# Walking the streamed operand of an MLP's matmuls in interleaved pieces

## Chip, cores and metric

The kernel runs on one core of a Trainium2 chip. The metric is the device time of one execution in microseconds. Two executions of the kernel before took 1046.23 and 1046.22 us, median 1046.22 us. Besides these there is one profiled execution, from which all rows come.

## What is computed

A trunk of two layers over 512 tokens with 1024 features, in float32. Layer 0 mixes by multi-head latent attention, layer 1 by gated linear attention; each mixer is followed by an MLP with a squared ReLU, and every part adds to the residual stream.

```
def sq_relu_mlp(xn, w_up, w_down):          # w_up 1024 x 4096, w_down 4096 x 1024
    hid = jnp.square(jax.nn.relu(xn @ w_up))
    return hid @ w_down

for i in range(2):
    x = x + mixer_i(rms_norm(x, norm_mix[i]))
    x = x + sq_relu_mlp(rms_norm(x, norm_mlp[i]), mlp_w_up[i], mlp_w_down[i])
return rms_norm(x, final_norm)
```

The change touches the MLP alone, in both layers.

## The kernel before

*Numbers in two parts.* Each float32 operand is split into a high part, which the matmul's input type holds, and a low part, the rest. A product is then three matmuls: high by high, high by low and low by high. ScalarE makes the high part (line 110), VectorE the low one (line 113); for weights both are called from `piece`, which writes them to the tiles `wh` and `wl`.

*Steps.* The 4096 hidden features of an MLP are taken in eight blocks of 512. The first block's hidden values are made by `up_first`. Then seven steps follow, b = 0 to 6: step b makes the hidden values of block b + 1 (the up products) and multiplies those of block b by their part of `w_down` (the down products). The last block's down product comes after the loop. Step 0 is `step`, which alternates up and down products; steps 1 to 6 are `step_in_halves`, which makes all up products first and then all down products.

*Seven products in place of eight.* Each block product of 2 by 2 quarters is made by seven quarter products of sums and differences of quarters, which VectorE, ScalarE and the accumulating DMAs form. So a step has seven calls of `up_product` and seven of `down_product`.

*`up_product`* (line 956 on) holds a quarter of `w_up` in the array, 128 columns at a time, and streams 256 tokens of the activations past it: two halves j, four k, three terms, 24 matmuls of 256 columns, all issued in line 962. The sums of half j lie in columns j x 256 and on of one bank of the sums' memory.

*`down_product`* (line 965 on) holds 128 tokens of the hidden values and streams 512 columns of `w_down`: two groups of tokens, two k, three terms, 12 matmuls of 512 columns, all issued in line 971. The sums fill one bank each.

In each matmul call the second argument is the operand that is held in the array (its load is a row of its own in the profile, PEld), and the third is the one that is streamed. The names after the arrow in a profile row have the streamed one first. Until now every streamed row and every row of sums was walked from its first column to its last.

*Order of the work.* TensorE runs its matmuls in the order of the program. The loads of `w_up` and `w_down` for the next step are issued by `fetch` on SyncE's queue, and for sums of two quarters on GpSimd's queue as well (lines 949 and 951), at places that `after` marks. Elsewhere in the program, the attention of layer 1 scales rows in place in groups of 1, 2, 4 and so on elements (line 1492, over the view `crossing` of line 1480) and copies such views (line 1541); these are among the rows that the prediction uses for comparison.

Of the kernel before, what the change touches and what calls it, by code (L numbers as in the profile page):

```python
# [50 lines left out]
def trunk_kernel(ctx: ExitStack, tc: tile.TileContext, t_in: dict, out: bass.AP):  # L51
    nc = tc.nc
    PE, ACT, DVE, POOL, SP = nc.tensor, nc.scalar, nc.vector, nc.gpsimd, nc.sync
# [22 lines left out]
    def bank(tag):  # L76
        return psum["pool"].tile([P, 512], F32, tag=f"ps_{tag}", bufs=psum["banks"][tag], name=uname("ps"))
# [72 lines left out]
    def piece(raw, a, n, order=lambda i: i, at=(W_AT, W_AT)):  # L150
        hi = room_for("wh", a, n, at[0])
        lo = room_for("wl", a, n, at[1])
        split(raw, hi, lo, order=order)
        return hi, lo

    def cut(pair, *idx):
        return tuple(t[idx] for t in pair)
# [657 lines left out]
    def mlp(layer, nrm, nxt=None):  # L815
# [3 lines left out]
        KH = ND // 2  # L819
# [112 lines left out]
        def fetch(b, name):  # L932
            if name in ("A1", "A2"):
                c = int(name[1]) - 1
                if c == 0:
                    W[name] = col_chunk(w_up, (b + 1) * FB, 256)
                    return None
                W[name] = t = sb.tile([P, ND, 256], F32, tag="wraw", bufs=2, name=uname("wraw"))
                SP.dma_start(t[:, :KH], up_quadrant(b, 1, 0))
                POOL.dma_start(t[:, :KH], up_quadrant(b, 0, 0), accum_op=ALU.add)  # L940
                SP.dma_start(t[:, KH:], up_quadrant(b, 1, 1))
                return None
            q = up_quadrant if name == "S1" else down_quadrant
            W[name] = t = by_k(comb(home[name]), KH if name == "S1" else 2)
            plain, more = {
                "d11": ((0, 0), None), "d12": ((0, 1), None), "d22": ((1, 1), None),
                "S1": ((1, 1), (1, 0)), "dS1": ((1, 1), (1, 0)), "dS3": ((1, 0), (0, 0)),
            }[name]
            first_part = SP.dma_start(t, q(b, *plain))
            if more:  # L950
                POOL.dma_start(t, q(b, *more), accum_op=ALU.add)
            return first_part

        def up_product(t, a, q, start):
            w = piece(a, KH, 256, at=AT_UP)
            for j in range(2):
                o = t[:, j * TH : (j + 1) * TH]
                for k in range(KH):
                    wh, wl = cut(w, slice(None), k, slice(j * P, (j + 1) * P))
                    xh, xl = quad[q][k][:, 0], quad[q][k][:, 1]  # L960
                    for n, (a_, x_) in enumerate(((wh, xh), (wh, xl), (wl, xh))):
                        PE.matmul(o, a_, x_, start=start and j == 0 and k == 0 and n == 0, stop=k == KH - 1 and n == 2, skip_group_check=True)  # L962

        def down_product(t, a, parts, start):
            wh, wl = piece(a, 2, 512)
            for tt in range(2):
                o = t[tt] if isinstance(t, list) else t[:, tt * 512 : (tt + 1) * 512]
                for k in range(2):
                    xh, xl = cut(parts, slice(None), slice(k * TH + tt * P, k * TH + (tt + 1) * P))
                    for n, (x_, w_) in enumerate(((xh, wh[:, k]), (xh, wl[:, k]), (xl, wh[:, k]))):  # L970
                        PE.matmul(o, x_, w_, start=start and k == 0 and n == 0, stop=k == 1 and n == 2, skip_group_check=True)  # L971


        def step(b, q, r, after):
# [14 lines left out]
            def onto(tag, total, a, parts, fresh=False):  # L989
                t = two_banks(tag)  # L990
                if not fresh:
                    ACT.activation(t, total, AF.Copy)
                down_product(t, a, parts, fresh)
                ACT.activation(total, t, AF.Copy)
# [4 lines left out]

            z = bank("u")  # L1000
            up_product(z, a11, "11", True)
            y = bank("u")
            ACT.activation(y, z, AF.Copy)

            d = two_banks("d")
            down_product(d, d11, parts_of_quad(q11), True)
            if opening:
                ACT.activation(S11, d, AF.Copy)
            e = two_banks("e") if opening else begun(d)

            up_product(y, a12, "21", False)
            finish(y, 0, 0, r)
            DVE.tensor_tensor(a11, s1, a11, ALU.add)

            down_product(e, d12, parts_of_quad(q21), opening)
            DVE.tensor_tensor(S11, e, S11, ALU.add)
            DVE.tensor_tensor(d11, ds1, d11, ALU.add)
# [11 lines left out]
            def up_t2():  # L1029
                up_product(z, a11, "T2", False)  # L1030
                u = part["u"] = tmp()
                ACT.activation(u, z, AF.Copy)
                DVE.tensor_tensor(a12, a11, a12, ALU.add)
# [147 lines left out]
        def before_next(name):  # L1181
            if name in ("d11", "S1", "d12", "dS3"):
                t = by_k(comb(home[name]), 2)
                SP.dma_start(t, x_kept[:, 2 * len(kept) : 2 * len(kept) + 2])
                kept.append(t)
            if name in ("A1", "A2"):
                last_raw.append(load(down_cols(len(last_raw)), 4, 512))
            if name == "dS1":
                DVE.tensor_tensor(S12, S12, S5, ALU.add)

        def at_the_end(name):
            if name in ("d11", "S1", "d12", "dS3"):
                i = len(last_raw)
                t = by_k(comb(home[name]), 2)
                k0 = (NB - 1) * FB + i % 2 * 256
                SP.dma_start(t, w_dn[k0 : k0 + 256, i // 2 * 512 : (i // 2 + 1) * 512].rearrange("(k p) n -> p k n", p=P))
                last_raw.append(t)
            if name == "dS1":
                DVE.tensor_tensor(S12, S12, S5, ALU.add)
                t = comb(home[name])  # L1200
                SP.dma_start(t, t_in["fin_row"].to_broadcast([P, D]))
                gain.append(t)
                rounded(0)

        for b in range(NB - 1):
            final = b == NB - 2

            def after(name, b=b, final=final):
                if final:
                    return before_next(name) if nxt else at_the_end(name)  # L1210
                fetch(b + 1, name)

            (step_in_halves if b else step)(b, Q[b % 2], Q[(b + 1) % 2], after)

        q = Q[(NB - 1) % 2]
        if nxt:
# [6 lines left out]
            for c in range(2):  # L1223
# [5 lines left out]
                for j, p in enumerate(ps_):  # L1229
                    for t in range(NT):  # L1230
                        o = t % 2 * 512 + j * P
# [26 lines left out]
        for c in range(2):  # L1258
            for th in (1, 0):
                total = (S11, S12, S21, SU)[2 * c + th]  # L1260
                if c == 0:
# [3 lines left out]
                    o = loaded[th]  # L1265
                for i in range(2):
                    cs = slice(i * 512, (i + 1) * 512)
                    if c:
                        o = bank("u")
# [529 lines left out]
    n_mix1 = Norm(ND, inv_dr, "mix", ND)  # L1799
    psum_layout("quad")  # L1800
    mlp(0, n_mlp0, n_mix1)
    psum_layout(False)
    Y, begun = gla(0, n_mix1, "B", "B")
# [3 lines left out]

    psum_layout("quad")
    mlp(1, n_mlp1)


# [46 lines left out]
```

## Time and profile before

| | |
|---|---|
| median of the runs | 1046.22 us |
| profiled execution, span from first to last instruction | 1044.9 us |
| middle steps of layer 0 (steps 1 to 6) | 245.9 to 474.8 us of the span |
| middle steps of layer 1 (steps 1 to 6) | 785.9 to 1015.0 us of the span |
| one middle step | 38.16 us, twelve of them |

The page gives busy time by engine; PE is TensorE's matmuls, PEld its loads of the held operand, DVE VectorE, ACT ScalarE, POOL GpSimd, and a q behind an engine's name its queue. The slices cut the span in 40 equal parts with the busy share in tenths. The chain is the work that ended last, followed back from the end. Matmuls overlap in the array, so the duration of a single row (390 ns for 512 columns, 275 ns for 256) is longer than the distance from one matmul to the next; the distance is read from the starts, or from how long a run of many takes.

### The profile page before, as it was taken

The page shows a single profiled execution, that of the slowest core. Times are in us where ns is not written, and L with a number is a line of the kernel's source. Part 1 is how long each engine was busy: PE and PEld are TensorE (multiplying, and loading weights), DVE is VectorE, ACT ScalarE, POOL GpSimd, SP SyncE. Part 2 cuts the span into 40 slices and gives each one's busy share as a digit, 9 for nine tenths or more (in the row PEclk, how much of TensorE's full clock was granted, in tenths as well). Part 3 has the DMA queues.
Part 4 walks back from the last instruction along what each step waited for, and adds up shares of the span by engine and source line. Part 5 has one row for each costly group of instructions (what it writes and reads, how often), then busy time and mean ns, then how long its engine had stood idle before and what let it go on. Part 6 is the DMA issues. An engine that isn't in the chain of part 4 may idle for free.

```text
span 1044.9 us, 15747 instructions
## 1 busy us (share of the span) xinstructions
PE 1035.0 (99%) x5966; PEld 903.9 (87%) x5966; DVE 876.9 (84%) x1340; ACT 696.8 (67%) x1122; POOL 114.3 (11%) x128
## 2 busy tenths in 40 slices
PE   9999999999999999999999999999999999999997
PEld 8788888899899899898888888888889989989986
DVE  7889977988989989989687399469798999898993
ACT  8667754577776776785445566555677677677784
POOL 8400010301101101000000000000011111110000
PEclk9999999999999999999999999999999999999999
DMA  7401235769878778644212222165488778778422
GB/s 232 122 21 41 81 95 147 224 166 215 216 191 202 178 203 202 161 136 126 77 55 82 87 74 75 48 162 147 95 241 201 185 202 198 194 191 191 111 81 81
DMA packets 120717, 149.98 MB, mean 144 GB/s; under 512 B 9568, under 2 KB 86368, under 8 KB 120512
## 3 DMA queue, kind: packets, MB, share of 16 engines
q1 hardware_dynamic: 96144, 117.76, 35.4%
q0 software_dynamic: 22400, 29.36, 18.0%
q10 hardware_dynamic: 2096, 1.84, 0.6%
q8 instruction: 47, 0.77, 0.3%
q14 instruction: 30, 0.25, 0.1%
HBM read 144.49 MB, written 4.19 MB: 142 GB/s over the span
## 4 chain that ended last, share of the span: by engine, by line
PE 94%; DVE 3%; ACT 2%; issue 0%; DMA 0%; ACTq 0%; SPq 0%; DVEq 0%
PE ps L971 25%; PE ps L962 25%; PE ps L118 10%; PE ps L120 10%; PE ps L119 10%; PE ps L1279 2%; PE ps L1240 2%; PE ps L1499 1%; PE ps L135 1%; PE ps L421 1%; PE ps L1626 1%; DVE wl L113 1%; PE ps L1766 0%; PE ps L1549 0%; PE ps L684 0%
## 5 line engine op out<-in xcount | busy, mean ns | idle before, releaser
L971 PE MATMUL ps<-wh,set 128*128 128x512 f32 x784 | 245.7, 390 | 0.3 <-ACT set L110 0.3
L110 ACT ACTIVATE wh<-wraw 128x1024 fp32r<-128x1024 f32 x139 | 146.4, 1056 | 110.2 <-PE ps L119 42.6
L113 DVE TENSOR_TENSOR wl<-wraw,wh 128x1024 fp32r<-128x1024 f32 x139 | 169.7, 1222 | 39.0 <-ACT wh L110 38.7
L971 PEld LDWEIGHTS ps<-wh,set 128*128 128x128 f32 x784 | 147.0, 188 | 30.7 <-ACT set L110 0.7
L962 PE MATMUL ps<-T,wh 128*128 128x256 f32 x896 | 154.9, 275 | 0.0
L971 PE MATMUL ps<-wl,set 128*128 128x512 f32 x392 | 152.6, 389 | 0.0
L113 DVE TENSOR_TENSOR wl<-comb,wh 128x1024 fp32r<-128x1024 f32 x112 | 136.8, 1221 | 18.5 <-ACT wh L110 18.3
L110 ACT ACTIVATE wh<-comb 128x1024 fp32r<-128x1024 f32 x112 | 118.3, 1057 | 47.6 <-issue 28.7
L962 PEld LDWEIGHTS ps<-T,wh 128*128 128x128 f32 x896 | 135.4, 188 | 0.4
L962 PE MATMUL ps<-T,wl 128*128 128x256 f32 x448 | 123.4, 275 | 0.0
L962 PE MATMUL ps<-set,wh 128*128 128x256 f32 x672 | 117.1, 276 | 0.0
L118 PE MATMUL ps<-set,wh 128*128 128x512 f32 x280 | 109.7, 392 | 0.0
L119 PE MATMUL ps<-set,wh 128*128 128x512 f32 x280 | 109.6, 392 | 0.0
L120 PE MATMUL ps<-set,wl 128*128 128x512 f32 x280 | 109.3, 391 | 0.0
L962 PEld LDWEIGHTS ps<-set,wh 128*128 128x128 f32 x672 | 102.6, 188 | 1.3
L962 PE MATMUL ps<-set,wl 128*128 128x256 f32 x336 | 92.7, 276 | 0.0
L971 PEld LDWEIGHTS ps<-wl,set 128*128 128x128 f32 x392 | 73.6, 188 | 14.7
L962 PEld LDWEIGHTS ps<-T,wl 128*128 128x128 f32 x448 | 84.1, 188 | 0.1
L962 PEld LDWEIGHTS ps<-set,wl 128*128 128x128 f32 x336 | 63.1, 188 | 0.0
L120 PEld LDWEIGHTS ps<-set,wl 128*128 128x128 f32 x280 | 52.6, 188 | 11.1
L119 PEld LDWEIGHTS ps<-set,wh 128*128 128x128 f32 x280 | 52.6, 188 | 11.1 <-DVE set L750 0.2
L118 PEld LDWEIGHTS ps<-set,wh 128*128 128x128 f32 x280 | 52.6, 188 | 10.7
(415 smaller groups left out, 2015.4 us busy)
## 6 DMA issues: line engine op xcount, KB each, us to landing
comb<-in_mlp_w_down_dram SPq DMA_DIRECT2D x74, 512.0 KB, 4.1
wraw<-in_mlp_w_up_dram SPq DMA_DIRECT2D x18, 1024.0 KB, 5.6
comb<-in_mlp_w_down_dram POOLq DMA_DIRECT2D x28, 512.0 KB, 6.5
wraw<-in_mlp_w_up_dram SPq DMA_DIRECT2D x28, 512.0 KB, 5.6
wraw<-in_gla_w_in_dram SPq DMA_DIRECT2D x12, 1024.0 KB, 5.2
comb<-in_mlp_w_up_dram SPq DMA_DIRECT2D x14, 512.0 KB, 4.4
comb<-in_mlp_w_up_dram POOLq DMA_DIRECT2D x14, 512.0 KB, 6.4
wraw<-in_mlp_w_up_dram POOLq DMA_DIRECT2D x14, 512.0 KB, 7.6
```

The lines of the kernel that those rows point to most:

```text
L110: order(ACT.activation(hi, src, AF.Copy))
L113: lo_eng.tensor_tensor(lo, src, f(hi), ALU.subtract)
L118: PE.matmul(psum, wh, xh, start=start, stop=False)
L119: PE.matmul(psum, wh, xl, start=False, stop=False)
L120: PE.matmul(psum, wl, xh, start=False, stop=stop)
L135: PE.transpose(psum, src, ident[: src.shape[0], : src.shape[0]])
L421: PE.matmul(p, w[:, i, j * P : (j + 1) * P], x, start=start, stop=stop)
L962: PE.matmul(o, a_, x_, start=start and j == 0 and k == 0 and n == 0, stop=k == KH - 1 and n == 2, skip_group_check=True)
L971: PE.matmul(o, x_, w_, start=start and k == 0 and n == 0, stop=k == 1 and n == 2, skip_group_check=True)
L1240: PE.matmul(p, a, x, start=False, stop=k == 3 and n == 2, skip_group_check=True)
L1279: PE.matmul(o, a, b_, start=False, stop=k == 3 and n == 2, skip_group_check=True)
L1499: PE.matmul(p[:, t - t0], k[:, t * P : (t + 1) * P], moving[:, t], start=True, stop=True)
```

## The change

A view `streamed` is put around the streamed operand and around the sums of both lines. With a pair (h, c) it cuts the row of N columns into h equal stretches and each stretch into N / (h c) pieces of c columns; the walk goes over the pieces in the outer loop, over the h stretches inside that, and over the c columns innermost. With the empty pair it leaves the row as it is. Each step sets its pair before it starts: step 0 has the empty one, steps 1 to 6 of layer 0 have (2, 16), (2, 32), (2, 8), (2, 4), (4, 16), (2, 64), and steps 1 to 6 of layer 1 have (4, 8), (8, 4), (8, 8), (8, 32), (2, 128), (16, 8).

```
+        ORDERS = (((), (2, 16), (2, 32), (2, 8), (2, 4), (4, 16), (2, 64)), ((), (4, 8), (8, 4), (8, 8), (8, 32), (2, 128), (16, 8)))[layer]
+        order = [()]
+
+        def streamed(ap):
+            if not order[0]:
+                return ap
+            h, c = order[0]
+            return ap.rearrange("p (h i c) -> p i h c", h=h, c=c)
+
         def up_product(t, a, q, start):
...
-                        PE.matmul(o, a_, x_, start=start and j == 0 and k == 0 and n == 0, stop=k == KH - 1 and n == 2, skip_group_check=True)
+                        PE.matmul(streamed(o), a_, streamed(x_), start=start and j == 0 and k == 0 and n == 0, stop=k == KH - 1 and n == 2, skip_group_check=True)
 
         def down_product(t, a, parts, start):
...
-                        PE.matmul(o, x_, w_, start=start and k == 0 and n == 0, stop=k == 1 and n == 2, skip_group_check=True)
+                        PE.matmul(streamed(o), x_, streamed(w_), start=start and k == 0 and n == 0, stop=k == 1 and n == 2, skip_group_check=True)
...
+            order[0] = ORDERS[b % len(ORDERS)]
             (step_in_halves if b else step)(b, Q[b % 2], Q[(b + 1) % 2], after)
```

The held operand of both lines, and every instruction outside them, is as before. The sums of each matmul land in the same places as before, since both views are walked alike.

## The prediction

> **What bounds the kernel now.** I read the page from the top: busy time by engine, the granted clock, then the chain that ended last.
>
> ```profile
> span 1044.9 us, 15747 instructions
> PE 1035.0 (99%) x5966; PEld 903.9 (87%) x5966; DVE 876.9 (84%) x1340; ACT 696.8 (67%) x1122; POOL 114.3 (11%) x128
> PEclk9999999999999999999999999999999999999999
> PE 94%; DVE 3%; ACT 2%; issue 0%; DMA 0%; ACTq 0%; SPq 0%; DVEq 0%
> PE ps L971 25%; PE ps L962 25%; PE ps L118 10%; PE ps L120 10%; PE ps L119 10%; PE ps L1279 2%; PE ps L1240 2%; PE ps L1499 1%; PE ps L135 1%; PE ps L421 1%; PE ps L1626 1%; DVE wl L113 1%; PE ps L1766 0%; PE ps L1549 0%; PE ps L684 0%
> ```
>
> TensorE is never without work, its clock is granted in full, and half of the chain runs through exactly two lines, L962 (the up products) and L971 (the down products). These are the two lines that the change edits. Whatever the new walk does to one of their matmuls goes into the end time without a cover.
>
> Next I asked for the chain of waits over the middle steps of the first layer, steps 1 to 6.
>
> ```profile
> by line: PE ps L971 50.1%; PE ps L962 50.0%
> 245.86 19.09 PE ps L962 x168
> 264.95 19.07 PE ps L971 x84
> 284.02 19.09 PE ps L962 x168
> 303.11 19.07 PE ps L971 x84
> 322.18 19.09 PE ps L962 x168
> ```
>
> A step is one unbroken run of 168 matmuls of 256 columns and then 84 of 512 columns; the next starts 38.16 us later (284.02 to 322.18). No other engine appears in this stretch. So the price of a column is the whole question. From these rows: 19.09 us / 168 = 113.6 ns for 256 columns and 19.07 us / 84 = 227.0 ns for 512, which is 0.443 ns for a column in both.
>
> The windows, one step each, say how near the others are (columns: stretch, sum, then busy time of PE, PEld, DVE, ACT, POOL, clock, DMA share, GB/s).
>
> ```profile
> core 0: us, PE busy (x) PEld busy (x) DVE busy (x) ACT busy (x) POOL busy (x), PEclk, DMA share, GB/s
> 283.85:322.00 38.15, 38.15 (x253) 34.85 (x252) 35.03 (x39) 28.25 (x40) 3.75 (x3) 1.00 0.79 193
> 322.00:360.15 38.15, 38.15 (x253) 34.85 (x252) 35.03 (x39) 28.25 (x39) 4.98 (x4) 1.00 0.76 196
> 862.20:900.40 38.20, 38.20 (x254) 34.87 (x253) 35.09 (x39) 28.30 (x40) 4.60 (x5) 1.00 0.78 193
> ```
>
> TensorE fills the step, VectorE has 35.03 of 38.15 us, ScalarE 28.25. A slower TensorE would give the others slack and meet no second bound. A faster one would meet VectorE after 3.1 us a step.
>
> **The change part by part.** Step 0 of each layer has the empty order and is as before. Steps 1 to 6 of both layers, twelve in all, get one pair (h, c) each. The row of N columns is cut into h stretches, and the walk takes c neighbouring columns of the first stretch, c of the second, and so on, then the next c of each. The streamed operand and the sums are walked alike, so every product lands where it did, and every sum receives its terms in the same order.
>
> *Instructions, waits, queues.* Nothing is added or removed: 252 matmuls and their weight loads a step, the same shapes, the same DMAs, no queue moved past. The weights that are loaded aren't walked otherwise; only the streamed side is. A strided view covers exactly the half bank (L962) or bank (L971) of the plain one, and what follows reads the bank after its product has ended. So I cost this at 0 us. If a wait were put at a wrong place after all, every microsecond of it would show, since TensorE has no idle time to lose it in; against that stands that nothing in the set of read and written addresses changes.
>
> *Jumps inside a matmul.* This is the only cost in question. A step streams 168 x 256 + 84 x 512 = 86,016 columns, so it has 86,016 / c pieces. At c = 4 these are 21,504, at 8 10,752, at 16 5,376, at 32 2,688, at 64 1,344. Layer 0 has c = 16, 32, 8, 4, 16, 64: 47,040 pieces. Layer 1 has c = 8, 4, 8, 32, 128, 8; in its steps with (8, 32) and (2, 128) a 256-column row is exactly filled by h x c, so L962 is walked as before, and only the 84 down products count there: 1,344 and 336. That gives 55,440. Together 102,480 pieces in 2,688 matmuls, so 102,480 - 2,688 = 99,792 jumps inside a matmul.
>
> No row of this profile has a matmul that streams a broken row; all patterns there are unbroken. I bound a jump from three sides.
>
> The nearest row is a jump that TensorE makes already: the start of a matmul, which moves to another streamed address and, where the product goes on to its other half, to other sums. L962 and L971 stream the same 43,008 columns a step, the one in 168 starts, the other in 84. They take 19.09 and 19.07 us. The 84 additional starts cost 0.02 us together, at most 0.24 ns each. A jump at this price makes 99,792 x 0.24 ns = 24 us; at the lower end it is 0.
>
> The second bound is one column's time, 0.443 ns: a start can be prepared while the matmul before is running, a jump inside one perhaps can't. That is 99,792 x 0.443 ns = 44 us.
>
> The third rows are walks in pieces on the other engines.
>
> ```profile
> L1492 DVE TENSOR_TENSOR qk<-qk,T 128x512 f32<-128x512 f32 x28 | 19.0, 686 | 0.5 <-ACT E L1541 0.5
> L1149 DVE TENSOR_TENSOR set<-set,set 128x512 f32<-128x512 f32 x12 | 8.3, 692 | 0.4
> L1541 ACT ACTIVATE E<-qk 128x512 f32<-128x512 f32 x8 | 5.0, 626 | 2.6 <-DVE qk L1492 2.3 <-PE ps L1549 0.3
> L844 ACT ACTIVATE set<-set 128x512 fp32r<-128x512 f32 x42 | 26.3, 626 | 19.2 <-PE ps L971 19.1
> ```
>
> L1492 walks 512 elements in pieces of 1, 2, 4 and so on to 64 (seven levels of four heads, 28 in all) and takes 686 ns; L1149 walks 512 unbroken ones in 692. L1541 reads pieces of 32 and 64 in 626 ns, L844 an unbroken row in 626. On both engines a jump costs nothing that can be seen, even with single elements. These engines need 626 / 512 = 1.2 ns and more for an element where TensorE has 0.443, so their reads and writes have more time for a jump; the rows speak for zero, they don't prove it at TensorE's pace.
>
> I take 0 for the jump: the start row is nearest in engine and pace, and its 0.02 us is as much as the rounding of two rows gives.
>
> *Below nothing.* A walk in another order could also raise the pace, if 0.443 ns were set by how addresses follow each other. In these rows nothing points there: two shapes of matmul from several rooms have the same pace, in steps with 193 and 196 GB/s alike. The end on that side is VectorE's 35.03 us: 12 x (38.15 - 35.03) = 37 us less.
>
> *A rule against the change.* The Trainium skill, Advanced Engine Details and Errata, section Memory Cachelines, says of the sums' memory that any pattern that isn't contiguous slows matmuls significantly, and in its next line that every two neighbouring elements should be contiguous for best throughput, with lines of 8 bytes there and of 16 bytes in the operands' memory. By its first line all 2,688 matmuls would be slower, by its second none, as every piece has at least four neighbours of 4 bytes. No run here shows a broken row, so the trace can't decide between them yet.
>
> *Sum.* 0 + 0 us on the profiled execution's span of 1044.9 us. The runs' median of 1046.22 us lies 1.3 us over that span, for what surrounds it. Forecast 1046.2 us.
>
> **The rivals.**
>
> *A small price for a jump*, up to the 0.24 ns of the start row: up to 24 us, 1046 to 1070 us. For it: the rounding leaves it open. Against it: the pieces on VectorE and ScalarE.
>
> *A full column for each jump* (this is the case on the other side of the forecast). The stream would lose one column's time wherever its address isn't the next one: 44 us, 1090 us. Its place is in the twelve steps, its mark is 1/c: a step with c = 4 gains 21,252 x 0.443 = 9.4 us and takes 47.6, with c = 8 it gains 10,500 x 0.443 = 4.7 us, with c = 64 half a microsecond. It decides (2%, 21 us) from 0.21 ns a jump. For it: TensorE streams without any slack, so there is no cover. Against it: starts come for free.
>
> *Delivery in groups.* If columns are delivered in neighbouring groups of eight, a piece of four pays as much as one of eight: the two steps with c = 4 double, 2 x 38.16 = 76 us, 1122 us; nothing happens at c of 8 and more. With groups of sixteen c = 8 would double as well and c = 4 take four times as long, far above that. For it: nothing measured. Against it: L1492 pays nothing for single elements.
>
> *All broken rows slow.* If a broken row alone, whatever its c, halves the pace, then 1,680 up products (ten steps) at 113.6 ns and 1,008 down products at 227.0 ns count twice: 191 + 229 = 420 us, 1466 us. This is a mechanism of the row's form and not of the count of jumps, and the (8, 32) and (2, 128) steps would be spared in their up half alone. The first line of the Trainium skill's rule above would come to this, if significantly means half.
>
> *Faster.* The twelve steps fall towards VectorE's 35.03 us: at most 37 us, 1009 us. To pass 2% each step has to lose 1.75 us of 38.15. For it: VectorE leaves that room. Against it: nothing shows that the walk sets the pace. In the Trainium skill, TensorE: Matmul & The Clock Gate, section Back-to-back issue gap and the measurements ahead of it, 512 columns take 215.7 ns warm; by this the 227.0 ns here would leave 11.3 ns, an estimate of 11.4 us for the down products of the twelve steps and as much for the up products, 23 us.
>
> That the change doesn't do what it says is hardly a rival: only two of the twelve up halves keep their old order, and they are counted above.
>
> **How the numbers follow.** No effect: 0.50, time 1046.2, its own range 1041 to 1051. A small price: 0.13. A full column: 0.18. Groups: 0.10. All broken rows slow: 0.04. Faster: 0.05. A measurement of this kernel can tell about 2% from no change, so 1025.3 to 1067.1 us counts as the same. The small price lies there for about half of its chance. Same: 0.50 + 0.06 = 0.56. Slower: 0.07 + 0.18 + 0.10 + 0.04 = 0.39. Faster: 0.05. For the range I leave out the groups, the slow broken rows and the faster case (0.19 together) and take in the rest: from 1040 to 1095 us.
>
> **What would show it.** Right: in the chain of the middle steps 168 matmuls take 19.09 us and 84 take 19.07 in every one of them, and a step starts 38.16 us after the last. The two counts at 1/c tell the rivals apart: a full column gives 47.6 us at c = 4 and 42.8 at c = 8; groups give 76 us at c = 4 and 38.16 at c = 8; slow broken rows give the same time for c = 4 and c = 64, and 19.09 us for the up halves of the steps with (8, 32) and (2, 128). If the busy shares of VectorE rise with a shorter step, it was the pace. If idle time of TensorE appears, with a releaser named in front of L962 or L971, then costing the waits at nothing was wrong. What would make the forecast wrong is a price of a jump above 0.21 ns, which no row here measures directly.

## The result and the profile after

The changed kernel takes 1073.48 us (median of 1072.96 and 1074.00), against 1046.22 before: 1.0263 times, with a 95% interval of 1.0233 to 1.0293. It is 27.3 us slower. The page of the profiled execution, in the same lines as the one shown of before:

```profile
span 1071.3 us, 15757 instructions
PE 1062.1 (99%) x5966; PEld 918.5 (86%) x5966; DVE 881.5 (82%) x1340; ACT 698.6 (65%) x1122; POOL 113.9 (11%) x128
PEclk9999999999999999999999999999999999999999
PE ps L980 26%; PE ps L971 25%; PE ps L118 10%; PE ps L120 10%; PE ps L119 10%; PE ps L1289 2%; PE ps L1250 2%; PE ps L1509 1%; PE ps L135 1%; PE ps L421 1%; PE ps L1636 1%; DVE wl L113 1%; PE ps L1559 0%; PE ps L684 0%; ACT wh L110 0%
```

TensorE is still never without work, its clock is granted in full as before, and no other engine has begun to make it wait: the same matmuls, on the same two lines (now 971 and 980), only take longer. Where, the chain of waits tells for each step; the columns are start, length, line and count. Layer 0, with (2, 16), (2, 32), (2, 8), (2, 4), (4, 16), (2, 64):

```profile
246.08 20.54 PE ps L971 x168
266.62 20.16 PE ps L980 x84
286.78 20.02 PE ps L971 x168
306.80 19.88 PE ps L980 x84
326.69 21.27 PE ps L971 x168
347.95 20.44 PE ps L980 x84
368.39 21.40 PE ps L971 x168
389.79 21.02 PE ps L980 x84
410.81 20.36 PE ps L971 x168
431.17 19.43 PE ps L980 x84
450.60 19.07 PE ps L971 x168
469.67 19.08 PE ps L980 x84
```

And from layer 1 the steps with (4, 8), (8, 4) and (2, 128):

```profile
799.99 21.50 PE ps L971 x168
821.50 19.43 PE ps L980 x84
840.93 20.24 PE ps L971 x168
861.17 23.37 PE ps L980 x84
...
964.86 19.10 PE ps L971 x168
983.96 19.07 PE ps L980 x84
```

The six steps of layer 0 take 242.67 us (246.08 to 488.75) in place of 6 x 38.16 = 228.96, those of layer 1 242.57 (799.99 to 1042.56). That is 13.7 and 13.6 us, together 27.3: the whole loss lies here. Three things don't fit a price of a jump. Pieces of 64 columns cost nothing at all, with three and seven jumps to a matmul. At h = 2 the extra time of a 512-column matmul grows only from 10 ns (c = 32, 15 jumps) to 23 ns (c = 4, 127 jumps). And the same c = 4 costs the down products 1.95 us a step with h = 2 and 4.30 us with h = 8.

### The profile page after: what moved, and what is told of

Read it like the earlier page. It is cut to its first block, busy times and chain, and to the rows that moved or that the text cites. A ratio compares the mean times of both kernels' runs of the same rounds, so it can differ in the third digit from the quotient of the medians.

```text
span 1071.3 us, 15757 instructions
## 1 busy us (share of the span) xinstructions
PE 1062.1 (99%) x5966; PEld 918.5 (86%) x5966; DVE 881.5 (82%) x1340; ACT 698.6 (65%) x1122; POOL 113.9 (11%) x128
## 4 chain that ended last, share of the span: by engine, by line
PE 94%; ACT 2%; DVE 2%; DMA 1%; issue 0%; SPq 0%; ACTq 0%; DVEq 0%
PE ps L980 26%; PE ps L971 25%; PE ps L118 10%; PE ps L120 10%; PE ps L119 10%; PE ps L1289 2%; PE ps L1250 2%; PE ps L1509 1%; PE ps L135 1%; PE ps L421 1%; PE ps L1636 1%; DVE wl L113 1%; PE ps L1559 0%; PE ps L684 0%; ACT wh L110 0%
## 5 line engine op out<-in xcount | busy, mean ns | idle before, releaser
L980 PE MATMUL ps<-wh,set 128*128 128x512 f32 x784 | 255.4, 403 | 0.3 <-ACT set L110 0.3
L971 PE MATMUL ps<-T,wh 128*128 128x256 f32 x896 | 162.7, 283 | 0.0
L980 PE MATMUL ps<-wl,set 128*128 128x512 f32 x392 | 157.7, 402 | 0.0
L971 PEld LDWEIGHTS ps<-T,wh 128*128 128x128 f32 x896 | 138.3, 189 | 0.4
L971 PE MATMUL ps<-T,wl 128*128 128x256 f32 x448 | 126.6, 282 | 0.0
L971 PE MATMUL ps<-set,wh 128*128 128x256 f32 x672 | 122.4, 283 | 0.0
L971 PEld LDWEIGHTS ps<-set,wh 128*128 128x128 f32 x672 | 104.7, 189 | 1.6
L971 PE MATMUL ps<-set,wl 128*128 128x256 f32 x336 | 95.0, 283 | 0.0
L110 ACT ACTIVATE set<-set 128x512 fp32r<-128x512 f32 (+1 forms) x70 | 42.6, 608 | 35.5 <-PE ps L980 33.2
L119 PEld LDWEIGHTS ps<-set,wh 128*128 128x128 f32 x280 | 52.6, 188 | 11.1 <-DVE set L750 0.2
```

The costliest lines, as they stand in the source:

```text
L110: order(ACT.activation(hi, src, AF.Copy))
L119: PE.matmul(psum, wh, xl, start=False, stop=False)
L971: PE.matmul(streamed(o), a_, streamed(x_), start=start and j == 0 and k == 0 and n == 0, stop=k == KH - 1 and n == 2, skip_group_check=True)
L980: PE.matmul(streamed(o), x_, streamed(w_), start=start and k == 0 and n == 0, stop=k == 1 and n == 2, skip_group_check=True)
```

## The experiments

### Which side pays

Two kernels walk only one of the two patterns in pieces.

```
e1:  PE.matmul(o, a_, streamed(x_), ...)            PE.matmul(o, x_, streamed(w_), ...)
e2:  PE.matmul(streamed(o), a_, x_, ...)            PE.matmul(streamed(o), x_, w_, ...)
```

> Lines 971 and 980 walk only the streamed operand in pieces; the sums are written from first to last column, so results land in other places than the reference's. With the full change the twelve steps took 27.3 us more than before (layer 0: 40.7, 39.9, 41.7, 42.4, 39.8, 38.2 us for the steps with 2,16 / 2,32 / 2,8 / 2,4 / 4,16 / 2,64; layer 1: 40.9, 43.6, 41.3, 39.0, 38.2, 39.5 for 4,8 / 8,4 / 8,8 / 8,32 / 2,128 / 16,8). If the price is paid where the streamed operand is read: the same steps, +27 us. If it is paid where the sums are written: every step 38.16 us, +0. If each side pays its own part, in between; if the price is one for a broken pattern in the instruction, whichever side, +27 here and +27 with the sums alone.

> Lines 971 and 980 walk only the sums in pieces; the operand is streamed from first to last column, so results land in other places than the reference's. If the price is paid where the sums are written: the steps of the full change, +27 us. If it is paid where the streamed operand is read: every step 38.16 us, +0.

Measured, a single time each: 1074.07 us with the streamed operand alone in pieces, 1045.50 with the sums alone; before, on the same chip, 1045.73. The chain of the step with (2, 4), first of the kernel that walks the operand, then of a step of the kernel that walks the sums:

```profile
368.61 21.40 PE ps L971 x168
390.00 21.02 PE ps L980 x84
```

```profile
283.87 19.09 PE ps L971 x168
302.95 19.07 PE ps L980 x84
```

The operand alone pays the full price: each step of layer 0 is as in the changed kernel to a hundredth of a microsecond. The sums pay none; the steps of both layers stand at 19.09 and 19.07 us throughout. The Trainium skill's first line on the sums' memory (Advanced Engine Details and Errata, section Memory Cachelines: any pattern that isn't contiguous slows matmuls significantly) doesn't hold for these patterns; its second line, that every two neighbours should be contiguous, agrees with them, as every piece has four columns or more; sums in smaller pieces were not run.

### Whether the unit is 16 bytes, and whether the held operand has a part

Three kernels keep the walk of the change. One takes every second column of 256 as the held operand in place of 128 neighbours; two move the start of every streamed row by two and by four words, with the held operand where it was.

```
e3:  wh, wl = cut(w, slice(None), k, slice(j, 2 * P, 2))                 # up
     ... slice(k * TH + tt, (k + 1) * TH, 2)                             # down
e4:  X_AT 44 -> 46; room of T 4 -> 6; down: piece(a, 2, 512, at=(126, 126))
e5:  X_AT 44 -> 48; room of T 4 -> 8; down: piece(a, 2, 512, at=(124, 124))
```

> As the changed kernel, but the held operand of lines 971 and 980 takes every second column of 256 in place of 128 neighbours (the halves j and the token groups tt are mixed up, so results differ from the reference's). If the price comes from the streamed walk meeting the loads of the held operand in the same memory, the steps change: other extra times per step than 2.5, 1.7, 3.5, 4.3, 1.6, 0 and 2.8, 5.5, 3.2, 0.8, 0, 1.4 us, and the steps that are walked as before may move away from 38.16. If it comes from the streamed walk or the sums alone, the steps stay as in the changed kernel within 0.2 us.

> As the changed kernel, but every streamed operand of lines 971 and 980 starts two words (8 bytes) later, so that a piece of four columns is no longer one 16-byte unit but touches two. If what counts is how many 16-byte units a piece touches, the steps with 4 columns (42.4 and 43.6 us) rise most, by up to the time that they would take with pieces of 2; those with 8 columns rise by less and (2,64) by next to nothing. If only the number of jumps or their stride counts, all steps stay within 0.2 us.

> As the changed kernel, but every streamed operand of lines 971 and 980 starts four words (16 bytes) away from where it was, with the held operands in their old places. If what cost 161 us with two words was that a piece of four columns straddles two 16-byte units, it is gone here: the steps with 4 columns come back from 56.3 and 78.1 us (168 and 84 matmuls at 168.9 and 332.2 ns, at 222.2 and 486.0 ns) to within 2 us of the changed kernel's 42.4 and 43.6. If any move of the streamed row against the held one costs that, they stay near 56 and 78. In the steps walked as before (2,128 and the first step) the row moved against the held one costs about 3% by the groups measured alone (227 to 233 ns for 512 columns), so 38.16 becomes 39 to 40 us; if only broken rows pay, it stays 38.16.

Measured, a single time each: 1080.29, 1234.27 and 1077.43 us. The chain of the moved rows, steps with (2, 4) and (2, 128), two words:

```profile
403.82 28.37 PE ps L971 x168
432.19 27.90 PE ps L980 x84
...
1105.36 20.17 PE ps L971 x168
1125.53 20.26 PE ps L980 x84
```

four words, the same steps with (4, 8) between them:

```profile
367.23 21.30 PE ps L971 x168
388.52 20.72 PE ps L980 x84
...
801.11 19.79 PE ps L971 x168
820.90 21.20 PE ps L980 x84
...
967.89 19.88 PE ps L971 x168
987.77 19.87 PE ps L980 x84
```

With two words the (2, 4) step takes 56.3 us, with four 42.0, so 16 bytes is the unit. With a unit of 8 the first move would have been free. With one of 32 the pieces of 8 would straddle either with the second move or without it; but the down products of (2, 8) take 20.45 us with it and 20.44 in the changed kernel (29.75 with two words). What cost most of the 161 us was that every piece straddled one unit more than it fills. My expectation that pieces of 8 would suffer less than those of 4 was wrong: the (2, 8) step takes 59.8 us, and the four steps with pieces of 8 rose by 74.6 us together, the two with pieces of 4 by 48.4, so the count of units alone doesn't give the price.

Two more things go against a price of the broken row by itself. Look at (2, 128), whose up products are walked unbroken: they take 20.17 and 19.88 us in place of 19.10. A plain row slows down as well when it moves against the held one. And the move by four words changes a broken order both ways: at (4, 8) the up products fall from 21.50 to 19.79 us and the down products rise from 19.43 to 21.20, with the same jumps and the same units. The held operand's part shows in the first of the three kernels, at the step with (2, 128):

```profile
970.56 20.16 PE ps L971 x168
990.72 19.60 PE ps L980 x84
```

The streamed rows of this step are as before, only the held columns are read two apart, and a matmul takes some 6 ns longer whether it streams 256 columns (20.16 / 168 = 120.0 ns) or 512 (19.60 / 84 = 233.3). An addition that is the same for both lengths fits the one load of a held operand that each matmul has, and not the number of columns. The steps that paid most in the change hardly moved in this kernel, though ((2, 8) 41.72 us against 41.71, (2, 4) 42.26 against 42.42): it shows the held operand's part in unbroken rows alone.

### The matmuls alone

Two kernels hold nothing but groups of 48 matmuls, a source line for each group, with no other engine or transfer at work. The operands are float32r, the input type of the kernel's matmuls, unless another type is named. The place of a row is where it starts, in bytes past a multiple of 256.

```
for i in range(48): PE.matmul(PS[:, :512], HT[:, 8 + 512 * (i % 3) : 136 + 512 * (i % 3)],
    ST[:, 8 + 1024 * (i % 2) : 520 + 1024 * (i % 2)].rearrange("p (h i c) -> p i h c", h=32, c=4), ...)
```

> Only the matmuls are left: groups of 48 float32r matmuls in a row, one source line for each group, on constant data, no other engine or transfer at work; nothing of the reference is computed. Groups differ in the start of the streamed row and of the held one (in bytes past a 64-byte boundary), in the number of held columns (128, 96, 72), in their step, in the pair (h, c) and in the stride between stretches. If other engines' traffic is part of the price, the unbroken 512 columns (start 32, held 32) take less than the 227 ns that they take in the full kernel; if not, 227, and the pairs 2,16 / 2,8 / 2,4 the 240, 243 and 250 ns of the full kernel. If the price of a broken row comes from the held operand's loads in the same memory, 72 held columns in place of 128 take off about 44% of the excess over 227; if it is the streamed read's alone, nothing. If the stride decides (stretches whose addresses agree in their low bits meet in one part of the memory), 260, 264, 272, 288 and 320 columns between stretches give other times than 256; if the number of jumps decides, they give the same.

In order, the chain of the first one shows 512 columns unbroken with both starts at the same place (L64), unbroken with the streamed row 32 bytes on (L68), then with equal starts (2, 2), (2, 4), (2, 16), (8, 4), (32, 4) and (64, 4):

```profile
18.86 10.88 PE PS L64 x48
...
63.26 11.19 PE PS L68 x48
...
219.21 16.01 PE PS L82 x48
235.21 12.00 PE PS L83 x48
...
258.89 11.52 PE PS L85 x48
...
496.78 13.34 PE PS L105 x48
...
521.94 10.86 PE PS L107 x48
532.80 11.10 PE PS L108 x48
```

Divided by 48 these are 226.7, 233.1, 333.5, 250.0, 240.0, 277.9, 226.3 and 231.3 ns. The full kernel's down products come back (250.2 for (2, 4), 278.2 for (8, 4)), ten of the twelve orders within half a nanosecond in this kernel or the next, so other engines and transfers aren't needed for the price. The two others, (8, 8) with 258.5 ns in the kernel and (16, 8) with 230.6, have more than one time alone too, as will be seen. The places of the up products were not copied, and their times come back less well ((2, 64): 113.5 ns in the kernel, 116.9 alone).

The number of jumps falls as a theory: (2, 4), (8, 4), (32, 4) and (64, 4) all have 127 jumps in a matmul and take 250, 278, 226 and 231 ns, the third as little as no jump at all. The stride between the stretches matters with pieces of 4 (240 to 251 ns for 260 to 320 columns) and not with pieces of 16 (240.0 throughout). With 72 held columns in place of 128, (2, 4) falls from 250.0 to 246.7 and (2, 16) stays at 240.0, while the unbroken row rises from 226.7 to 230.4. Against 226.7 that takes 14% and nothing off the excess, against the unbroken row of the same width 30 and 28%: neither the 44% that a mere count of meetings would have taken off nor, clearly, nothing. Nor do equal starts fix the time of an unbroken row: with both rows at 16 bytes it was 231.0 ns (L77).

> As the run with the matmuls alone, with other groups; nothing of the reference is computed. If the number of jumps sets the price, 32 or 64 stretches with pieces of 4 take what (2,4) takes, 250 ns (the run before had 226.7 and 231.1, so this should fall again with pieces of 8 and with 256 columns). If the order of the 16-byte units against the held operand's loads sets it, the time of an unbroken row changes with the held row's start also by 64 bytes and more, and some broken order may be below 226.7 and 113.3 ns. If the price comes with the bytes that a column takes, bfloat16 rows (2 bytes) of 512 columns pay nothing for pieces of 8, 16 and 32; if it comes with the columns, they pay the same 10 to 17 ns. float32 rows, which TensorE streams at half the pace, should pay nothing with pieces of 8 and 16 if the price is a matter of bytes in time.

From the second kernel: 256 columns unbroken with the held row at the same place (L86) and 64 bytes on (L90), (16, 8) for 512 (L105), bfloat16 unbroken, in pieces of 4 and of 8 (L130, L131, L132), float32 of 256 columns unbroken and in pieces of 8 (L135, L137, two passes each):

```profile
195.92 5.76 PE PS L86 x48
...
218.78 5.45 PE PS L90 x48
...
319.73 10.56 PE PS L105 x48
...
564.14 10.38 PE PS L130 x48
574.51 10.88 PE PS L131 x48
585.39 10.36 PE PS L132 x48
616.47 20.72 PE PS L135 x96
657.91 20.72 PE PS L137 x96
```

An unbroken row of 256 columns takes 120.0 or 113.5 ns, with nothing changed in the matmul but the place of the held row, and for 512 columns the times repeat when that place moves by 256 bytes (226.7, 233.3, 232.5, 229.0 ns for 0, 64, 128, 192, then 227.1, 233.3, 232.5, 229.0, and twice more). A broken row can be faster than an unbroken one: (16, 8) takes 220.0 ns. And of the three types only float32r paid for whole units: bfloat16 takes 216 ns unbroken and with pieces of 8, 16 and 32, and pays only where a piece of four columns is half a unit (226.7); float32, at half the pace (215.8 ns for 256 columns in each pass), pays for nothing with pieces of 4, 8 and 16. These groups had two stretches and equal starts alone, and both operands had the type, so whether the streamed or the held side makes the difference isn't shown.

A third kernel of this kind put seven orders of 256 and five of 512 columns at sixteen places of the held row.

> As the runs with the matmuls alone, 28 matmuls to a group; nothing of the reference is computed. Seven broken orders for 256 columns and five for 512, each with the held row in sixteen places of a 256-byte period. If the price is one of the jumps, no place of the held row changes an order's time. If it is set by how the streamed row's 16-byte units meet those of the held row, each order has places 3 to 10% apart, and some of them are below the unbroken row's 226.7 and 113.3 ns, as (16,8) was with 220.0; a floor is then the 213.3 and 106.7 ns that 512 and 256 columns would take without any meeting, an estimate from the 16/17 by which 226.7 exceeds it in the groups of float32 and bfloat16 rows (215.8).

Eight of the twelve orders have places 3% and more apart, (8, 8) for 512 columns most (231 to 263 ns); (64, 4) for 512 columns and (16, 4), (8, 16) and (32, 4) for 256 differ by 1 to 3%. None of the orders for 256 columns is clearly below 113.3 ns, and 220 is the floor for 512, at a few places. For (16, 8) and (32, 4) the sixteen places were run again with both rows 64 bytes on: 31 of these 32 groups came back within 0.4 ns, so what counts, at least for moves by 64 bytes, is the place of the one row against the other. The exception shows why even a table of places won't always do. (16, 8) with equal starts took 220.0 ns in the second kernel, at the same addresses; here it is run first (L70) and, with both rows 64 bytes on, once more (L150):

```profile
14.21 6.45 PE PS L70 x28
...
543.16 6.20 PE PS L150 x28
```

These are 230.4 and 221.4 ns. In the single distances L70 runs in a round of 228, 229, 230, 230, 237; L150, after its first two, alternates between 219 and 221, as the group of the second kernel did almost from its start. (8, 8) with equal starts, too, settles at 233 ns in the second kernel and at 263 here. The matmuls settle into a rhythm, and the same order at the same places has more than one. These pairs of groups differ in what ran ahead of them, so that is likely what picks the rhythm; no run varied it alone.

### More jumps than the change, and faster

Three kernels go from the kernel before, all with unbroken up products. One walks all down products, step 0 included, as (32, 4) (e8), one moves their streamed row from word 128 to word 72, which is 32 bytes on in a period of 256 (e7), one does both (e6).

```
+ def walked(ap): return ap.rearrange("p (h i c) -> p i h c", h=32, c=4)          # e6, e8
+ PE.matmul(walked(o), x_, walked(w_), ...)                                       # e6, e8
+ wh, wl = piece(a, 2, 512, at=(72, 72))                                          # e6, e7
```

> The kernel before, with the down products of all seven steps of both layers walked as (32, 4), and the streamed row moved to start 32 bytes past the held one in a period of 256. 127 jumps in each of 84 matmuls in 14 steps, 149,352, half as many again as the change has. If a jump costs (27.3 us for 99,792, 0.27 ns each), this is 40 us slower than before, 1086 us. If the meeting of the streamed and the held reads decides, this place gave 219.9 ns with the matmuls alone: 7 ns less for each of 1,176 matmuls, 8 us faster than before, 1038 us; if the lock falls into another of its rhythms (223 to 231 ns were seen), 1042 to 1051.

> The kernel before, with the streamed row of the down products moved by 32 bytes against the held one and walked unbroken. If only broken rows pay, 227.1 ns for a down matmul and the time of before, 1046 us. If the meeting decides, 233.3 ns as alone at this place: 6.2 ns for each of 1,176 matmuls, 7 us slower, 1053 us.

> The kernel before, with the down products of all seven steps walked as (32, 4), starts as before. If a jump costs, 1086 us. If the meeting decides, 226.7 ns as alone at this place, and the time of before, 1046 us.

Measured: both together 1043.18 us, 0.9975 of before (0.9964 to 0.9985; 1045.63 us before in these rounds); the move alone 1052.11 and the walk alone 1043.86, a single time each. The chain of a step with both and of one with the move alone:

```profile
283.17 19.07 PE ps L962 x168
302.23 18.93 PE ps L974 x84
```

```profile
284.78 19.06 PE ps L962 x168
303.84 19.60 PE ps L971 x84
```

149,352 jumps, half as many again as in the change, and the kernel is 2.5 us faster than before, a quarter of a per cent. A price of a jump had said 1086 us. The move without the walk makes a down matmul 233.3 ns as it did alone, and the kernel 6.5 us slower, with not one broken row in it. The eight microseconds that were expected of both edits didn't come in full: in the kernel the down products settle at 18.93 / 84 = 225.4 ns, where this order at this place had 220.0 alone. The walk without the move has 19.03 / 84 = 226.5 ns, as expected; these matmuls account for 0.6 of the 1.8 us by which its one run is faster.

## Why the prediction was wrong

The forecast was 1046.2 us and no change that can be measured; the time is 1073.5. The range of 1040 to 1095 held it, through the rivals.

*What bounds the kernel* was right, and so was what follows from it: TensorE has no cover, and the whole loss went into the end time, 27.3 us in the two lines.

*Instructions, waits, queues at 0 us*: right. No idle time of TensorE appeared in the steps, and no other engine entered their chain.

*Jumps inside a matmul at 0* is the step that failed, in its choice and in its form. I took the start of a matmul as the nearest row and let two equal halves (19.09 and 19.07 us) say that a new address is free. That row compares two unbroken rows that both ran near the best pace that unbroken rows showed (113.6 and 227.0 ns, against 113.3 and 226.7 alone); it can't speak for another order. It was also read too closely: two rows rounded to 0.01 us may differ by 0.03, 0.36 ns for a start, which would have put the upper bound at 36 us and not 24. And I bounded the price by the number of jumps, which isn't what it goes by: 127 jumps cost 0, 5, 23 or 51 ns by their stride, a piece of 64 columns costs nothing, and 149,352 jumps went with a gain. What stands in its place is a price of the order and of the places of the two rows: 0 to 5.5 us a step, 27.3 us in all.

*Below nothing*: I wrote that nothing pointed to a pace set by how addresses follow each other, because two shapes had the same 0.443 ns from several rooms. The runs show the contrary: 226.7 and 113.3 ns are the best that unbroken rows took here, and 233 and 120 come by moving a start. The lines with the starts (44, 124, 60, 128 words) were in the code; I never asked what the streamed and the held row's places did to each other.

*The rows of VectorE and ScalarE* were rightly called weak. These engines' pieces cost nothing, as did those of float32 on TensorE at half the pace; at full pace float32r paid.

*The rivals.* The small price came nearest in size (up to 24 us; 27.3 measured), but the (2, 64) steps and (32, 4) refute it as a mechanism, as they do the full column. Groups of eight would have doubled c = 4 and left c = 8 alone; c = 8 paid 41.71 - 38.16 = 3.55 us a step at h = 2, nearly as much as c = 4 with 4.26. Slow broken rows would have spared no c; (2, 64) is spared. Faster didn't happen: none of the twelve steps fell below 38.15 us.

*The rule that was weighed*, the Trainium skill's on the sums' memory, was weighed at the wrong memory: the sums could be walked in pieces for nothing (1045.50 us against 1045.73), and the price lies with the operands.

What the runs show, then, is that the time hangs on two reads at once: the streamed row, in units of 16 bytes, and the held row. The order of the units and the place of the one row against the other, in a period of 256 bytes, decide it, up to the rhythm that the matmuls fall into. That the two reads are in conflict for parts of one memory is my reading of this, not shown; a stream without any load of a held operand wasn't tried (a group with the same held row 48 times still loads it 48 times, and settles at 226.7 ns). What stays open is the rule by which an order gets its price: the times lie at steady rhythms (226.7, 233.3, 240.0), and the same addresses gave two of them.

## What to carry to other kernels

Where float32r matmuls run without a gap, the order and the start of the streamed row count against those of the held row, even for unbroken rows: measure a few groups of matmuls alone, which gave the down products of ten of the twelve orders to half a nanosecond, before changing either, and then the kernel, as an order can have more than one time. A row that shows one pattern near its best is no bound for another pattern. The sums could be walked in all twelve ways for nothing.

## What the runs showed that was not expected

- Moving all streamed rows of the changed kernel by 8 bytes cost 161 us (1234.27 against 1073.48), moving them by 16 bytes 4 us.
- Pieces of two columns take 333 ns for 512 columns, with (32, 2) 431 ns (the time for 48 is 20.7 us): units used by halves cost most. In the kernel moved by 8 bytes, where pieces of four use two halves, (8, 4) takes 486 ns.
- bfloat16 rows take 215.8 ns where unbroken float32r rows take 226.7 at best, 5% less, and were indifferent to the walks in two stretches whose pieces fill whole units. The 215.7 ns of the Trainium skill (TensorE: Matmul & The Clock Gate, section "Wait — 56ns, not 53.3ns?") agree with them; the float32r rows of 512 columns, 220.0 at their best here, didn't reach it.
